# Stores issued alternately by SP and ACT instead of all by SP

## The chip, the core and the metric

The kernel runs on one core of one Trainium2 chip. The metric is the device time of one execution in microseconds (us). A quoted time is the median of a kernel's runs. A quoted ratio is the mean time of one kernel's runs over that of the other's in the same rounds, so it is not quite the ratio of the medians.

The engines are named as the profile names them: PE multiplies, DVE and ACT copy, POOL issues the loads, SP issues stores. Each of these five has its own stream of instructions. Data moves between memory and the core on 16 DMA engines, which all the queues share; they move it in packets, and the trace has one record for each packet. PSUM is the buffer that PE writes its results to.

## The reference

For each of 96 (batch, head) pairs the scores are a product of a 1024x64 and a 64x1024 matrix:

```python
batch, n_heads, seq, head_dim = 8, 12, 1024, 64          # q, k: float32
def reference(q, k):
    return np.einsum('bhid,bhjd->bhij', q, k).astype(np.float32)
```

The inputs are 50 MB in all, the output 403 MB. It is a kernel that mostly writes.

## The kernel before

Heads are handled in batches of four (the first three batches are smaller). POOL loads q and k of a batch and converts them to 16 bits, three batches ahead; PE transposes them into PSUM; DVE copies the transposes out. For each head, 16 matmuls fill eight PSUM tiles, ACT copies five of them and DVE three into one output tile of 4 MB, and one store writes that tile.

```python
in_pool  = ctx.enter_context(tc.tile_pool(name="in_pool", bufs=4))
out_pool = ctx.enter_context(tc.tile_pool(name="out_pool", bufs=4))   # 4 x 4 MB
# ...
        def scores(self, g):
            bh = self.first + g
            # ...
            o_sb = out_pool.tile([P, NT, S], F32, tag="out")
            for t in range(NT):
                # ... two matmuls into ps (L106)
                if t in (1, 4, 6):
                    nc.vector.tensor_copy(out=o_sb[:, t], in_=ps)     # L112
                else:
                    nc.scalar.copy(out=o_sb[:, t], in_=ps)            # L114
            nc.sync.dma_start(                                        # L115
                out=of[bh].rearrange("(p t) j -> p (t j)", p=P),
                in_=o_sb.rearrange("p t j -> p (t j)"),
            )
# ...
        for g in range(b.G):
            b.scores(g)
            if nxt:
                for a in range(g * nxt.G // b.G, (g + 1) * nxt.G // b.G):
                    nxt.transpose(a)        # PE L78, L81, L82; DVE L91, L92
```

Of the kernel before, what the change touches and what calls it, by code (L numbers as in the profile page):

```python
# [1 line left out]

# [5 lines left out]


F16 = mybir.dt.float16  # L10
F32 = mybir.dt.float32
P = 128


@with_exitstack
def kernel(
    ctx: ExitStack,
    tc: tile.TileContext,
    q: bass.AP,
    k: bass.AP,  # L20
    out: bass.AP,
):
    nc = tc.nc

    B, H, S, D = q.shape
    NT = S // P
    BH = B * H
    GMAX = 4
    assert D == 64 and NT == 8 and BH % GMAX == 0





    qf = q.rearrange("b h s d -> (b h s) d")
    kf = k.rearrange("b h s d -> (b h s) d")
    of = out.rearrange("b h i j -> (b h) i j")

    sizes = [1, 1, 2] + [GMAX] * (BH // GMAX - 1)
    assert sum(sizes) == BH  # L40

    consts = ctx.enter_context(tc.tile_pool(name="consts", bufs=1))
    ident = consts.tile([P, P], F16)

    in_pool = ctx.enter_context(tc.tile_pool(name="in_pool", bufs=4))
    tr_pool = ctx.enter_context(tc.tile_pool(name="tr_pool", bufs=2))
    out_pool = ctx.enter_context(tc.tile_pool(name="out_pool", bufs=4))
    pt_pool = ctx.enter_context(
        tc.tile_pool(name="pt_pool", bufs=1, space=bass.MemoryType.PSUM)
    )  # L50
    po_pool = ctx.enter_context(
        tc.tile_pool(name="po_pool", bufs=3, space=bass.MemoryType.PSUM)
    )

    class Batch:
        def __init__(self, first, G):
            self.first, self.G, self.R = first, G, 8 * G

        def load(self):
            rows = slice(self.first * S, (self.first + self.G) * S)  # L60
            self.q_sb = in_pool.tile([P, GMAX * NT, D], F16, tag="q")
            self.k_sb = in_pool.tile([P, GMAX * NT, D], F16, tag="k")
            for src, dst in ((qf, self.q_sb), (kf, self.k_sb)):
                nc.gpsimd.dma_start(  # L64
                    out=dst[:, : self.R],
                    in_=src[rows].rearrange("(p r) d -> p r d", p=P),
                )

        def alloc(self):
            self.qT = tr_pool.tile([P, GMAX * 4 * P], F16, tag="qT")  # L70
            self.kT = tr_pool.tile([P, GMAX * S], F16, tag="kT")

        def transpose(self, a):
            G, pp = self.G, P // self.G
            t_ps = pt_pool.tile([P, 12, P], F16, tag="pt")
            for e in range(4):
                r = a * NT + 2 * e
                nc.tensor.transpose(t_ps[:, e], self.q_sb[:, r : r + 2], ident)  # L78
            for t in range(NT):
                rows = self.k_sb[:, a * NT + t]  # L80
                nc.tensor.transpose(t_ps[0:64, 4 + t], rows, ident)  # L81
                nc.tensor.transpose(t_ps[64:128, 4 + t], rows, ident)  # L82
            qT = self.qT[:, : G * 4 * P].rearrange(
                "c (g e m a) -> c g e m a", g=G, e=4, m=pp
            )
            kT = self.kT[:, : G * S].rearrange(
                "c (g m a t) -> c g m a t", g=G, m=pp, t=NT
            )
            for g in range(G):
                ms = slice(g * pp, (g + 1) * pp)  # L90
                nc.vector.tensor_copy(out=qT[:, g, :, :, a], in_=t_ps[:, 0:4, ms])  # L91
            nc.vector.tensor_copy(  # L92
                out=kT[:, :, :, a],
                in_=t_ps[:, 4:12].rearrange("c t (g m) -> c g m t", g=G),
            )

        def scores(self, g):
            bh = self.first + g
            qT = self.qT.rearrange("c (g e m) -> c g e m", e=4, m=P)
            kT = self.kT.rearrange("c (g j) -> c g j", j=S)  # L100
            o_sb = out_pool.tile([P, NT, S], F32, tag="out")
            for t in range(NT):
                h = (t % 2) * 64
                ps = po_pool.tile([P, S], F32, tag="po")
                for n in range(2):
                    nc.tensor.matmul(  # L106
                        ps[:, n * 512 : (n + 1) * 512],
                        qT[h : h + 64, g, t // 2],
                        kT[h : h + 64, g, n * 512 : (n + 1) * 512],
                    )  # L110
                if t in (1, 4, 6):
                    nc.vector.tensor_copy(out=o_sb[:, t], in_=ps)  # L112
                else:
                    nc.scalar.copy(out=o_sb[:, t], in_=ps)  # L114
            nc.sync.dma_start(  # L115
                out=of[bh].rearrange("(p t) j -> p (t j)", p=P),
                in_=o_sb.rearrange("p t j -> p (t j)"),
            )

    batches, first = [], 0  # L120
    for G in sizes:
        batches.append(Batch(first, G))
        first += G

    AHEAD = 3
    for b in batches[:AHEAD]:
        b.load()
    make_identity(nc, ident)
    batches[0].alloc()
    for a in range(batches[0].G):  # L130
        batches[0].transpose(a)
    for i, b in enumerate(batches):
        if i + AHEAD < len(batches):
            batches[i + AHEAD].load()
        nxt = batches[i + 1] if i + 1 < len(batches) else None
        if nxt:
            nxt.alloc()
# [4 lines that stand above are left out]
                    nxt.transpose(a)  # L142


# [1 line left out]
_INS = ['q', 'k']  # L146
_OUTS = [((8, 12, 1024, 1024), 'float32')]


# [23 lines left out]
```

## Time and profile before

| | before |
|---|---|
| time, median of 4 runs | 1071.33 us (1071.20 to 1072.24) |
| busy share of PE, DVE, ACT | 59%, 53%, 44% |
| DMA queues, share of the 16 engines' span | stores 88.0%, loads 11.9% |

The busy row of the DMA engines in 40 slices, in tenths (9 is 90% or more), and the traffic in each slice:

```profile
DMA  9999999999999999999999999999999999999996
GB/s 213 394 382 386 380 400 414 394 420 396 410 410 384 422 398 410 411 389 419 401 397 424 390 419 401 400 419 389 415 406 399 422 430 430 429 434 432 431 431 292
```

The DMA queues of the same page (packets, MB, share of 16 engines), and the issues by size with the median from issue to landing:

```profile
q1 hardware_dynamic: 13824, 402.66, 88.0%
q0 software_dynamic: 7488, 25.17, 11.9%
...
out_dram<-o_sb SPq DMA_DIRECT2D x96, 4096.0 KB, 36.7
q_sb<-in_q_dram POOLq DMA_DIRECT2D x23, 512.0 KB, 18.1
k_sb<-in_k_dram POOLq DMA_DIRECT2D x23, 512.0 KB, 29.4
```

And the list of waits (total us, times, longest):

```profile
ACT o_sb L114 <- DMA out_dram<-o_sb: 359.1, 87, 7.3
...
DVE o_sb L112 <- DMA out_dram<-o_sb: 213.8, 47, 7.5
ACT o_sb L114 <- PE ps L106: 207.0, 196, 8.9
DVE o_sb L112 <- PE ps L106: 158.8, 165, 2.5
```

Read together: queue q1 (SP's stores) and q0 (POOL's loads) fill the engines' time completely, 88.0% and 11.9%. The engines that compute wait for stores to free one of the four output tiles. A store takes about 10 us of the engines' time, yet 36.7 us from issue to landing, so more than three stores stand in line at any time. Only the last slice is not full. There is no gap that a second queue could fill.

### The profile page before, as it was taken

The numbers are of one execution on the slowest core, as the hardware profiler recorded it, in microseconds if no ns is written. First come the engines' busy times: TensorE is split into PE (matmuls) and PEld (weight loads), VectorE is DVE, ScalarE is ACT, GpSimd is POOL, SyncE is SP. The second block draws the span as 40 slices with busy tenths as digits, with TensorE's granted clock in tenths as the row PEclk, the third lists the DMA queues.
The fourth block names the chain that finished last, engine by engine and source line by source line (L and its number), as shares of the span: only waits on it lengthen the run. The fifth ranks groups of instructions, "written<-read, shape, count | busy, mean of one in ns | idle before, by whom it ended". The sixth has DMA issues, their size and how long they took to land.

```text
span 1069.6 us, 8844 instructions
## 1 busy us (share of the span) xinstructions
PE 627.9 (59%) x3456; PEld 214.0 (20%) x3456; DVE 565.7 (53%) x758; ACT 468.4 (44%) x481; POOL 28.2 (3%) x58
## 2 busy tenths in 40 slices
PE   6786455565654656557465564655656567667530
PEld 2222121121211212212122121221211212212100
DVE  5676445464653646547455464554655646655420
ACT  4454344444533445344443444444444445454530
POOL 3000000000000000000000000000000000000000
PEclk8565555555555555555555555555555555555555
DMA  9999999999999999999999999999999999999996
GB/s 213 394 382 386 380 400 414 394 420 396 410 410 384 422 398 410 411 389 419 401 397 424 390 419 401 400 419 389 415 406 399 422 430 430 429 434 432 431 431 292
DMA packets 21353, 428.39 MB, mean 401 GB/s; under 512 B 2368, under 2 KB 2880, under 8 KB 9024
## 3 DMA queue, kind: packets, MB, share of 16 engines
q1 hardware_dynamic: 13824, 402.66, 88.0%
q0 software_dynamic: 7488, 25.17, 11.9%
q8 instruction: 27, 0.44, 0.1%
q14 instruction: 14, 0.11, 0.0%
HBM read 50.33 MB, written 402.65 MB: 424 GB/s over the span
## 4 chain that ended last, share of the span: by engine, by line
DMA 77%; PE 7%; ACT 7%; DVE 1%; issue 0%; ACTq 0%
DMA out_dram<-o_sb 77%; ACT o_sb L114 7%; PE ps L106 6%; DVE kT L92 0%; DVE qT L91 0%; PE t_ps L81 0%; PE t_ps L78 0%; DVE o_sb L112 0%; PE t_ps L82 0%; ACTq L114 0%
## 5 line engine op out<-in xcount | busy, mean ns | idle before, releaser
L114 ACT COPY o_sb<-ps 128x1024 f32<-128x1024 f32 x480 | 467.1, 1014 | 566.5 <-DMA out_dram<-o_sb 359.1
L106 PE MATMUL ps<-kT,qT 64*128 64x512 f16 x1536 | 480.9, 597 | 270.8 <-ACT o_sb L114 227.2
L112 DVE COPY o_sb<-ps 128x1024 f32<-128x1024 f32 x288 | 351.7, 1223 | 374.0 <-DMA out_dram<-o_sb 213.8
L106 PEld LDWEIGHTS <-qT 64*128 64x128 f16 x1536 | 101.0, 109 | 605.2 <-issue 580.0
L91 DVE COPY qT<-t_ps 128x128 f16<-128x128 f16 (+1 forms) x374 | 121.2, 469 | 95.7 <-PE t_ps L82 95.7
L78 PE MATMUL t_ps<-ident,q_sb 128*128 128x128 f16 x384 | 56.4, 299 | 135.9 <-DVE kT L92 130.2
L92 DVE COPY kT<-t_ps 128x1024 f16<-128x1024 f16 x96 | 118.8, 1237 | 0.0
L81 PE MATMUL t_ps<-ident,k_sb 128*64 128x128 f16 x768 | 102.5, 310 | 0.0
L82 PE MATMUL t_ps<-ident,k_sb 128*64 128x128 f16 x768 | 102.4, 310 | 0.0
L81 PEld LDWEIGHTS <-k_sb 128*64 128x64 f16 x768 | 77.5, 165 | 19.8 <-issue 19.4
L82 PEld LDWEIGHTS <-k_sb 128*64 128x64 f16 x768 | 77.4, 164 | 7.5 <-issue 7.5
L78 PEld LDWEIGHTS <-q_sb 128*128 128x128 f16 x384 | 34.6, 127 | 187.2 <-issue 121.3
L64 POOL DMA_DIRECT2D q_sb<-in_q_dram x26 | 14.0, 537 | 767.5 <-PE t_ps L78 766.8
L64 POOL DMA_DIRECT2D k_sb<-in_k_dram x26 | 13.9, 534 | 13.2 <-PE t_ps L82 13.2
L114 ACT ACT_TABLE_LOAD x1 | 1.3, 1283 | 0.7 <-PEq L157 0.7
masks.py:199 POOL TENSOR_SCALAR_AFFINE_SELECT ident<-ident 128x128 f16<-128x128 f16 x1 | 0.4, 362 | 0.0
masks.py:197 POOL MEMSET ident<- 128x128 f16 x1 | 0.3, 271 | 0.0
L157 POOL MEMSET const-float32-0.0<- 128x1 f32 x1 | 0.1, 98 | 0.2 <-issue 0.2
L157 POOL MEMSET const-bfloat16-1.0<- 128x1 bf16 x1 | 0.1, 101 | 0.0
L157 POOL MEMSET const-uint8-127<- 128x1 uint8 x1 | 0.1, 101 | 0.0
L157 POOL MEMSET const-float32-1.0<- 128x1 f32 x1 | 0.1, 98 | 0.0
## 6 DMA issues: line engine op xcount, KB each, us to landing
out_dram<-o_sb SPq DMA_DIRECT2D x96, 4096.0 KB, 36.7
q_sb<-in_q_dram POOLq DMA_DIRECT2D x23, 512.0 KB, 18.1
k_sb<-in_k_dram POOLq DMA_DIRECT2D x23, 512.0 KB, 29.4
q_sb<-in_q_dram POOLq DMA_DIRECT2D x2, 128.0 KB, 3.5
k_sb<-in_k_dram POOLq DMA_DIRECT2D x2, 128.0 KB, 3.6
q_sb<-in_q_dram POOLq DMA_DIRECT2D x1, 256.0 KB, 6.3
k_sb<-in_k_dram POOLq DMA_DIRECT2D x1, 256.0 KB, 7.0
```

The lines of the kernel that those rows point to most:

```text
L64: nc.gpsimd.dma_start(out=dst[:, : self.R], in_=src[rows].rearrange("(p r) d -> p r d", p=P),)
L78: nc.tensor.transpose(t_ps[:, e], self.q_sb[:, r : r + 2], ident)
L81: nc.tensor.transpose(t_ps[0:64, 4 + t], rows, ident)
L82: nc.tensor.transpose(t_ps[64:128, 4 + t], rows, ident)
L91: nc.vector.tensor_copy(out=qT[:, g, :, :, a], in_=t_ps[:, 0:4, ms])
L92: nc.vector.tensor_copy(out=kT[:, :, :, a], in_=t_ps[:, 4:12].rearrange("c t (g m) -> c g m t", g=G),)
L106: nc.tensor.matmul(ps[:, n * 512 : (n + 1) * 512], qT[h : h + 64, g, t // 2], kT[h : h + 64, g, n * 512 : (n + 1) * 512],)
L112: nc.vector.tensor_copy(out=o_sb[:, t], in_=ps)
L114: nc.scalar.copy(out=o_sb[:, t], in_=ps)
L157: nc = _bacc.Bacc("TRN2", target_bir_lowering=False, num_devices=1)
```

## The change

The intent is to use the queues of two engines for the stores, so that two can be issued and served at once.

```diff
-            nc.sync.dma_start(
+            store = nc.sync if bh % 2 == 0 else nc.scalar
+            store.dma_start(
                 out=of[bh].rearrange("(p t) j -> p (t j)", p=P),
                 in_=o_sb.rearrange("p t j -> p (t j)"),
             )
```

(The copies keep their lines L112 and L114; the store is at L116 after the change.)

## The prediction

> **What bounds the kernel now: the DMA engines.** The row of the page by slices shows DMA at 9 (90% or more) in 39 of 40 slices. In the table by stretches its share is 0.99 to 1.07 from 10 us to 1050 us. The queue view gives stores 88.0% and loads 11.9% of the 16 engines' span: together all of it. The chain that ended last is 77% stores. PE is busy 59%, DVE 53%, ACT 44%; none sets the pace. In the list of waits, ACT waits 359 us and DVE 214 us for a store to free an output buffer. By the packet records, a store costs one engine eight packets of 32 KB at a median of 1.213 us plus a completion write, about 9.72 us. While only stores run (after 840 us) one ends every 9.7 to 9.8 us: no gap is left that a second queue could fill.
>
> **What the change moves.** 48 of the 96 stores of 4 MB go from SP's queue to ACT's; no bytes, packets, copies or matmuls change. SP's waits are 975 us for the DVE copy: it waits for data, not for its own issue cost, so no issue time is saved on the path. The Trainium skill, "DMA: Bandwidth & Descriptors", section "Issuing engines are not separate DMA queues", says that such DMAs "run on the same 16 DMA engines and interleave". This trace, with engines full from one queue, agrees as far as it goes.
>
> **What it adds.** ACT issues 48 stores in program order, each after the DVE copy of t=6. No trace here shows an issue on ACT[...]. A store takes about 11 us with its loads, ACT's copies 5 x 1.01 us of that, so it hides in ACT's wait for buffers.
>
> **The side effect.** Now up to two store queues compete with the load queue. A load pair (q and k, 1 MB) has 16 packets of 0.323 us per engine. Taking turns packet by packet (same page, "Queues, rings and completion order") with one store queue gives 16 x (1.213 + 0.323) = 24.6 us; the trace has 18.1 and 29.4 us to landing, which agrees. With two full store queues it is 16 x (2 x 1.213 + 0.323) = 44 us, about the time of four heads. So loads should land in 40 to 55 us, and the last of them later than 850 us. They are issued over two batches ahead (about 90 to 130 us), so PE should rarely wait; if it does, a store queue empties and the loads get its turn. The sum of work on the engines is unchanged.
>
> Two stores in flight each take twice as long in service but queue half as long; with four buffers the median from issue to landing stays near 36 us.
>
> **Predicted time.** Nearly 0 us of the path goes, nearly 0 is added: 1071 us, 8 in 10 between 1066 and 1077. Chances: faster by over 2%: 0.02; within 2%: 0.94; slower by over 2%: 0.04.
>
> **What would show it.** Right: DMA share still about 1.00 to 1050 us; two hardware queues with about 44% each; 32 KB packets still about 1.21 us; ACT and DVE waits for stores unchanged in sum; load landings longer. The last store's fastest and slowest engines end some 10 us apart before; a much different spread would move the end by a few us.
>
> **What would make it wrong.** Two regions 4 MB apart written at once slow the memory (32 KB packets over 1.25 us); loads starve so far that PE waits and the engines idle; ACT's issue blocks its copies; or a more even spread of the engines at the end saves up to 6 us.

## More of the kernel before

The framework that builds the kernel chooses the order of each engine's instructions itself. The order in the source is only a wish.

## The result, and the profile after

| | before | after |
|---|---|---|
| median, 4 runs each | 1071.33 us | 1075.07 us |
| lowest to highest | 1071.20 to 1072.24 | 1073.43 to 1077.38 |
| ratio, 95% interval | | 1.0035 (1.0015 to 1.0055) |
| profiled execution, span | 1069.6 us | 1071.7 us |

The change costs 0.35%, and the two ranges don't overlap. It is inside the predicted range and inside "within 2%", on its slow side. The profiled execution of the changed kernel was its fastest run, so its profile shows 2.1 us of the 3.7 us.

The same rows, queues and issues of the changed kernel:

```profile
DMA  9999999999999999999999999999999999999998
...
q10 hardware_dynamic: 6912, 201.33, 43.9%
q1 hardware_dynamic: 6912, 201.33, 43.8%
q0 software_dynamic: 7488, 25.17, 12.2%
...
out_dram<-o_sb SPq DMA_DIRECT2D x48, 4096.0 KB, 27.1
out_dram<-o_sb ACTq DMA_DIRECT2D x48, 4096.0 KB, 26.6
q_sb<-in_q_dram POOLq DMA_DIRECT2D x23, 512.0 KB, 25.4
k_sb<-in_k_dram POOLq DMA_DIRECT2D x23, 512.0 KB, 46.2
```

And its waits:

```profile
ACT o_sb L114 <- PE ps L106: 451.8, 258, 11.8
DVE o_sb L112 <- PE ps L106: 226.8, 188, 2.7
...
ACT o_sb L114 <- DMA out_dram<-o_sb: 121.2, 22, 8.2
DVE o_sb L112 <- DMA out_dram<-o_sb: 114.6, 21, 7.9
```

Four things differ. The stores are halved over q1 (SP) and q10 (ACT), as intended. Loads land much later (k in 46.2 us instead of 29.4). The same loads, with the same packets and bytes, take 12.2% of the engines' time instead of 11.9%. And stores land *sooner* after their issue, 27 us instead of 36.7, while ACT waits far less for stores and far more for PE: the line of waiting stores has become shorter.

The last point has a cause that the diff doesn't show. A look at how the compiled streams are ordered (fewer words, no times; x10 means ten of a kind in a row, T one group of transposes copied out) shows two moves in the changed kernel. In ACT's stream, most stores stand behind the *first copy of the next head*; in DVE's stream, three of the four transposes of a batch stand behind a copy of that next head, too:

```
ACT   after:   o_sb x10, store, o_sb x11, store, o_sb x10, store, o_sb x10, store ...
DVE   before:  o_sb x9,  T, T, o_sb x1, qT, o_sb x2, kT, T
DVE   after:   o_sb x10, (T split by one o_sb), o_sb x1, T, T, T       (T = qT copies and one kT copy)
```

A head has five copies on ACT, so from the second store on (after 21 copies, not 20) each store stands one copy late. That copy must wait for a free output tile. The timeline of ACT in the changed kernel (start us, us, what, and in brackets what its idle time waited for) shows a store held for it:

```profile
492.29 1.01 ACT L114 COPY o_sb<-ps 128x1024 f32<-128x1024 f32 x1 [0.93 <-PE ps L106]
497.42 1.01 ACT L114 COPY o_sb<-ps 128x1024 f32<-128x1024 f32 x1 [4.11 <-DMA out_dram<-o_sb]
497.49 0.34 ACTq L116 DMA_DIRECT2D out_dram<-o_sb  x1
```

The last copy of the head ends at 493.30. The store is issued at 497.49, because the next head's first copy stands ahead of it and waits 4.11 us for another store to land. The Trainium skill, "PSUM — Partial Sum Buffer", section "Engine vs sequencer instructions", says that ACT's queue is strictly first in, first out. It says so of the engine's own instructions; in this trace the store, which ACT's sequencer issues, keeps its place as well: it starts 0.07 us after the copy ahead of it has started. Of the 48 stores on ACT, 21 waited over 1 us in this way, 8.28 us at most; all 48 together waited 123 us. The issue itself takes 0.34 us.

DVE's timeline in the changed kernel, just after that, shows the transposes behind the same wait:

```profile
497.46 1.23 DVE L112 COPY o_sb<-ps 128x1024 f32<-128x1024 f32 x1 [3.78 <-DMA out_dram<-o_sb]
...
501.76 1.29 DVE L91 COPY qT<-t_ps 128x128 f16<-128x128 f16 x4 [0.55 <-PE t_ps L82]
502.85 1.25 DVE L92 COPY kT<-t_ps 128x1024 f16<-128x1024 f16 x1
505.80 1.29 DVE L91 COPY qT<-t_ps 128x128 f16<-128x128 f16 x4 [1.71 <-PE t_ps L82]
506.90 1.24 DVE L92 COPY kT<-t_ps 128x1024 f16<-128x1024 f16 x1
509.84 1.29 DVE L91 COPY qT<-t_ps 128x128 f16<-128x128 f16 x4 [1.70 <-PE t_ps L82]
510.94 1.25 DVE L92 COPY kT<-t_ps 128x1024 f16<-128x1024 f16 x1
514.90 1.23 DVE L112 COPY o_sb<-ps 128x1024 f32<-128x1024 f32 x1 [2.72 <-PE ps L106]
```

A head whose tile came free at 497.4 gets its last DVE copy only at 514.9. Counted over 30 to 1030 us, 3.31 stores were outstanding on average before and 2.52 after.

What that does to the DMA engines shows in the table by stretches, first of the changed kernel, then of the kernel before. (The columns after the stretch are busy us of each engine with counts, then the granted clock, the DMA share and GB/s. Loads count there with the 16-bit bytes they write, half of what they read.)

```profile
735.00:740.00 5.00, 4.02 (x16) 1.06 (x13) 2.45 (x2) 3.75 (x4) 0.00 (x0) 0.50 0.99 239
...
860.00:870.00 10.00, 4.99 (x46) 2.77 (x47) 5.57 (x11) 1.11 (x2) 0.00 (x0) 0.50 0.83 356
```

```profile
735.00:740.00 5.00, 3.17 (x10) 0.67 (x10) 1.75 (x2) 2.01 (x3) 0.00 (x0) 0.50 0.98 378
...
860.00:870.00 10.00, 6.53 (x21) 1.40 (x20) 4.41 (x4) 5.65 (x6) 0.00 (x0) 0.50 1.01 436
```

At 735 us the store queues have run almost dry, and most engines work on loads alone: still "busy", at 239 GB/s written instead of 378. At 860 us the last loads are in (861.7 us; 837.5 us before), so nothing fills such a gap any more and the engines idle: a share of 0.83.

The slow load packets of this kernel belong to the same gaps. Of its 3829 load packets that began between 150 and 800 us, 2200 began while fewer than 8 store packets were in flight on the 16 engines (before: 258 of 3807), and those took 339 ns in the mean; the ones that began beside 14 or more took 324 ns.

The packet records of the trace give the sum of it, per engine. Idle in mid-run (16 less the packets in flight, 30 to 1000 us): 2.7 us, before 0. The 4 KB load packets: a mean of 331.8 ns instead of 323.2, which over 368 of them per engine is 3.2 us. The 32 KB store packets: 0.7 us less. The idle at the end: 3.4 us less, because the first and the last engine to finish the last store are 4.4 us apart instead of 10.3. Together +1.8 us, of 2.1 in the spans.

So three suspects were on the table: the stores held in ACT's stream, the order of compute, and the two queues themselves.

### The profile page after: what moved, and what is told of

It reads as the page before. It is cut to its first block, busy times and chain, and to the rows that moved or that the text cites. A ratio compares the mean times of both kernels' runs of the same rounds, so it can differ in the third digit from the quotient of the medians.

```text
span 1071.7 us, 8793 instructions
## 1 busy us (share of the span) xinstructions
PE 662.2 (62%) x3456; PEld 217.8 (20%) x3456; DVE 569.8 (53%) x758; ACT 468.1 (44%) x481; POOL 28.3 (3%) x58
## 3 DMA queue, kind: packets, MB, share of 16 engines
q0 software_dynamic: 7488, 25.17, 12.2%
## 5 line engine op out<-in xcount | busy, mean ns | idle before, releaser
L114 ACT COPY o_sb<-ps 128x1024 f32<-128x1024 f32 x480 | 466.8, 1014 | 573.1 <-PE ps L106 451.8
L106 PE MATMUL ps<-kT,qT 64*128 64x512 f16 x1536 | 513.1, 604 | 218.2 <-ACT o_sb L114 138.2
L112 DVE COPY o_sb<-ps 128x1024 f32<-128x1024 f32 x288 | 350.2, 1222 | 369.2 <-PE ps L106 226.8
L106 PEld LDWEIGHTS <-qT 64*128 64x128 f16 x1536 | 104.3, 111 | 585.9 <-issue 578.6
L91 DVE COPY qT<-t_ps 128x128 f16<-128x128 f16 (+1 forms) x374 | 124.5, 466 | 102.5 <-PE t_ps L82 102.4
## 6 DMA issues: line engine op xcount, KB each, us to landing
q_sb<-in_q_dram POOLq DMA_DIRECT2D x23, 512.0 KB, 25.4
k_sb<-in_k_dram POOLq DMA_DIRECT2D x23, 512.0 KB, 46.2
```

The costliest lines, as they stand in the source:

```text
L91: nc.vector.tensor_copy(out=qT[:, g, :, :, a], in_=t_ps[:, 0:4, ms])
L106: nc.tensor.matmul(ps[:, n * 512 : (n + 1) * 512], qT[h : h + 64, g, t // 2], kT[h : h + 64, g, n * 512 : (n + 1) * 512],)
```

## The experiments

Each pair or group named together ran on one chip, with five rounds. The "32 KB" and "4 KB" columns of the tables are mean durations in ns of the store and the load packets that began between 150 and 800 us, from the packet records of the profiled execution.

### First job: is it the held stores?

E1, label e1_pinned: the changed kernel, with the next head's first ACT copy pinned behind the store.

```diff
-                    nc.scalar.copy(out=o_sb[:, t], in_=ps)
+                    c = nc.scalar.copy(out=o_sb[:, t], in_=ps)
+                    if t == 0:
+                        tc.keep_in_program_order(c)
```

> Stores alternate as in the change, but the next head's first ACT copy is pinned behind the ACT store, so that no finished store waits in ACT's stream for a free buffer (in the change 21 of 48 ACT stores waited over 1 us after their data was ready, 123 us in all; mean stores outstanding 2.5 against 3.3 before). Theory A (held stores let the DMA engines run dry): delay near 0, outstanding back to about 3.3, no idle engines between 800 and 1000 us (2.45 us in the change), and the time 1070 to 1072 us. Theory B (two store queues at once cost the engines something, mainly slower load packets, 3.2 us per engine more than before): the load packets keep a mean near 0.332 us and the time stays at 1074 to 1076 us. Both: about 1073.

E2, label e2_all_act: all stores on ACT, `store = nc.scalar`, held as they are.

> All 96 stores on ACT: one store queue again, but each store still sits behind the next head's first copy in ACT's stream. Theory A: many stores held for several us, outstanding near 2.5 or below, idle DMA engines, 1073 us or more. Theory B: one queue, so load packets back at 0.323 us and 1071 us, holds or not.

E3, label e3_all_act_pinned: E2 with the pin of E1.

> All 96 stores on ACT, each ahead of the next head's first copy: one queue and no hold. Both theories: as before, 1071 us within 1 us. A third theory, that ACT's issue of about 0.34 us itself costs time: above 1072.5 us, as there are twice as many of them as in the change.

E4, label e4_swapped: the changed kernel with `store = nc.scalar if bh % 2 == 0 else nc.sync`.

> As the change with the queues swapped: even heads on ACT, odd heads on SP. In the change the held stores were those of every fourth head (the last of a batch of four, an odd one); that one is now on SP. Theory A: few holds (under 30 us in all), outstanding over 2.8, time at most 1073 us. Theory B: 1074 to 1076 us as in the change, load packets near 0.332 us.

| | store queues | held in ACT, us in all | median us | ratio to before (95%) | 32 KB on SP, ACT | 4 KB |
|---|---|---|---|---|---|---|
| before | 1 | 0 | 1070.89 | | 1225, - | 322 |
| E1 pinned | 2 | 0 | 1076.48 | 1.0056 (1.0043 to 1.0068) | 1219, 1229 | 337 |
| E2 all ACT | 1 | 65 | 1070.13 | 0.9991 (0.9978 to 1.0005) | -, 1224 | 322 |
| E3 all ACT, pinned | 1 | 0 | 1071.77 | 1.0002 (0.9989 to 1.0014) | -, 1224 | 322 |
| E4 swapped | 2 | 181 | 1081.61 | 1.0093 (1.0080 to 1.0106) | 1230, 1246 | 323 |

("Held" leaves out the ordinary 0.03 us from data ready to issue.) Theory A, the held stores, falls. Without any hold E1 is as slow as the change or slower, and with holds but one queue E2 is as fast as before. The short line of stores is not the cause either: E2 and E3 have 2.42 and 2.44 stores outstanding, as few as E1 with 2.44. Nor is it ACT's issue: E3 has twice as many and costs nothing that can be measured. What E1 and E4 share, and E2 and E3 lack, is two store queues.

E1 and E3 are nearly a clean pair for an order about as late as the changed kernel's. Neither holds a store, their DVE streams agree in 747 of 758 places, and PE's differ by a few matmuls within each batch. E1, with two queues, takes 1076.18 to 1078.43 us; E3, with one, 1069.72 to 1072.63. Of E1's load packets between 150 and 800 us 2001 of 3834 began beside fewer than 8 store packets, of E3's 147 of 3840.

E4 was a surprise in size, +0.93%, and in its holds (under 30 us were expected). Its load packets were not slow, against what theory B said; its store packets were. Its loads landed in 91.1 (q) and 112.6 us (k). So two queues cost in two forms: slow load packets and gaps in the change and E1, slow store packets in E4.

### Second job: queues against order of compute

The order of PE's and DVE's instructions had changed in each of these kernels, since the framework reorders them whenever a store moves. So the next four kernels pin every matmul, transpose and DVE copy to the order of the source, and the compiled streams of PE and DVE are then the same in both kernels of a pair. In the "late" pair all four transposes of the next batch stand behind the copies t=0 and t=1 of the batch's first head, like in the changed kernel but more so; in the "even" pair one stands after each head, as the source has it.

```diff
+    K = tc.keep_in_program_order
-                nc.tensor.transpose(t_ps[:, e], self.q_sb[:, r : r + 2], ident)
+                K(nc.tensor.transpose(t_ps[:, e], self.q_sb[:, r : r + 2], ident))
     ... (the same around every matmul, transpose and DVE copy; ACT's t=0 copy as in E1)
# late pair only:
+                if t == 1 and nxt:            # in scores(), for the batch's first head
+                    for a in range(nxt.G):
+                        nxt.transpose(a)
# E5, E7:
-            store = nc.sync if bh % 2 == 0 else nc.scalar
+            store = nc.sync
```

> The order of PE's and DVE's instructions is pinned, the same in this kernel and the next: all four transposes of the next batch stand behind the copies t=0 and t=1 of a batch's first head, so they wait for an output buffer. All stores on SP. Theory C (two store queues served in turns land their stores in close pairs, so buffers come back late; this costs time only where the compute of the next head is also late, since then the engines run out of stores): one queue hides the late order, 1070 to 1072 us, outstanding stores near 2.4. Theory D (two store queues and the load queue in turns cost engine time whatever the compute order): also 1070 to 1072 us. A theory O, that the order of compute which the change brought along is the cause and the queues are not: 1074 us or more.

> As the kernel before it in this job, with stores alternating between SP and ACT; nothing else differs. Theories C and D: 1074 to 1079 us, engines idle or running on loads alone at each fourth head. Theory O: as the one-queue kernel of the same order, within 1 us.

> The order is pinned as the program is written: one transpose group after each head, so all heads take about the same time. All stores on SP. All theories: 1070 to 1072 us.

> The same even order, stores alternating. Theory C: heads come evenly, the store queues do not run dry, at most 1.5 us over the one-queue kernel of the same order. Theory D: 3 to 6 us over it, as with the late order. Theory O: the same as it.

| | order | store queues | median us (lowest to highest) | ratio to before (95%) | 32 KB on SP, ACT | 4 KB |
|---|---|---|---|---|---|---|
| E5 | late | 1 | 1070.98 (1068.34 to 1074.69) | 1.0004 (0.9988 to 1.0021) | 1226, - | 323 |
| E6 | late | 2 | 1073.02 (1072.19 to 1074.40) | 1.0019 (1.0007 to 1.0031) | 1220, 1229 | 334 |
| E7 | even | 1 | 1069.99 (1067.73 to 1072.72) | 0.9991 (0.9977 to 1.0005) | 1221, - | 323 |
| E8 | even | 2 | 1080.70 (1077.82 to 1083.89) | 1.0089 (1.0073 to 1.0105) | 1228, 1247 | 322 |

Theory O (order of compute alone) falls: with one queue the late and the even order both run as before. Theory C (paired landings need a late head to do harm) can't be the whole cause: the even order, where heads come regularly and 3.3 stores are outstanding on average, suffers most. For the late orders it is not excluded: there the engines do run short of stores (idle in mid-run 2.7 us in the change, 6.2 us in E1, 3.6 us in E6, against 1.0 us in E5). Theory D (the queues cost time whatever the order) fits best. E7 and E8 differ in nothing but the queue of every second store, and differ by 10.8 us (the means of their runs, 1069.93 and 1080.71). The late pair differs by 1.5 us in the mean, less than E5's own spread, so there the effect is not told from noise. E5's two longest runs, 1074.69 (the profiled one) and 1074.35 us, are also the two whose granted TensorE clock was high, 0.90 and 0.86 against 0.51 to 0.58; the other four average 1070.2 us. Whether the clock made them longer was not tested.

The DMA queues of E7:

```profile
q1 hardware_dynamic: 13824, 402.66, 88.0%
q0 software_dynamic: 7488, 25.17, 11.9%
...
q_sb<-in_q_dram POOLq DMA_DIRECT2D x23, 512.0 KB, 17.4
k_sb<-in_k_dram POOLq DMA_DIRECT2D x23, 512.0 KB, 28.5
```

and of E8:

```profile
q10 hardware_dynamic: 6912, 201.33, 44.3%
q1 hardware_dynamic: 6912, 201.33, 43.8%
q0 software_dynamic: 7488, 25.17, 11.8%
...
q_sb<-in_q_dram POOLq DMA_DIRECT2D x23, 512.0 KB, 75.0
k_sb<-in_k_dram POOLq DMA_DIRECT2D x23, 512.0 KB, 96.1
```

The engines are full in both, and none idles in mid-run. By the packet records the store queues take 938.7 us of each engine's time in E7 (88.0% of its span of 1066.8 us) and 948.4 us in E8 (88.1% of 1076.0 us). The same packets and bytes cost each engine 9.7 us more, and the span is 9.2 us longer. Most of the loss sits on ACT's queue: 476.6 us, where half of E7's stores take 469.4.

The packet records say which packets those are. In E8 between 150 and 800 us, 1113 of ACT's 3742 store packets took over 1233 ns, against 89 of SP's 3743, and 159 of 7588 in E7. Of the slow ones on ACT's queue, 99% ended within 12 ns of the start of a load packet; of ACT's ordinary ones 86% did so too. Of SP's ordinary packets, 89% ended where a packet of ACT's queue started. (A moment picked at random lies that close to such a start in some 13% of cases.) So the engines go round: SP's store packet, ACT's, a load packet, SP's again. The Trainium skill, "DMA: Bandwidth & Descriptors", section "Queues, rings and completion order", says that each engine takes its queues in turn, packet by packet, and the traces agree: k, issued 1 us after q, has 8 packets of its own on each engine, and it lands 12.2 us after q in E7, where 8 x (1.221 + 0.322) is 12.3 us, and 22.1 us after q in E8, where 8 x (1.228 + 1.247 + 0.322) is 22.4. Sixteen such rounds, 44.8 us for a load pair, are about the time of four heads (a pair lands every 44.7 us in E8, and every 44.1 us in E7 too). Loads in E8 get no more than their turn and it is just what they need, so about two pairs are in line and k lands in 96.1 us.

### Third job: take the loads away

If two streams of stores, 4 MB apart, simply disturbed each other in memory, they would do so without loads. These four kernels give wrong results: from the seventh batch on they use the inputs of the fourth to sixth again, so that most of the run has stores alone. (Twenty of the 26 pairs of loads are gone; the expectation says 18, which was a slip.)

```diff
         def load(self):
             rows = slice(self.first * S, (self.first + self.G) * S)
+            if self.first >= 16:
+                old = batches[3 + (self.first // 4 - 4) % 3]
+                self.q_sb, self.k_sb = old.q_sb, old.k_sb
+                return
```

(The input pool has six buffers instead of four, so that these inputs stay.)

> Wrong result on purpose: from the seventh batch on the inputs of the fourth to sixth are used again, so all loads end early (18 of 26 load pairs are gone) and the rest of the run has stores alone. Even order of compute, one store queue on SP. All theories: the stores' own time, 96 x 9.72 us plus start, early loads and end, about 975 us; 32 KB packets at 1.213 us.

> As the kernel before it, stores alternating (with loads this change of queue cost 9 us of span: 32 KB packets on ACT's queue took 1.239 us in the mean, nearly all slow ones just ahead of a load packet). Theory E (two store queues cost where they share the engines with loads): within 1.5 us of the one-queue kernel, packets at 1.213 us on both queues. Rival F (two store streams 4 MB apart slow each other at the memory, loads or not): 5 us or more slower.

> Without the later loads, late order of compute, one store queue. Stores alone have no loads to fill gaps: where a head comes late and fewer than two stores are left, engines idle. One queue: 975 to 985 us.

> As the kernel before it, stores alternating. Theory E alone: as the one-queue kernel within 1.5 us. If two stores served in turns also run dry together (landing in pairs, so that a buffer comes back later): 3 to 10 us slower, all of it as idle engines and none as slower packets.

| | order | store queues | median us (lowest to highest) | 32 KB on SP, ACT |
|---|---|---|---|---|
| E9 | even | 1 | 979.11 (978.98 to 979.35) | 1220, - |
| E10 | even | 2 | 979.33 (978.60 to 979.56) | 1220, 1220 |
| E11 | late | 1 | 991.11 (989.80 to 991.12) | 1221, - |
| E12 | late | 2 | 989.36 (989.19 to 989.78) | 1235, 1219 |

The DMA queues of E9:

```profile
q1 hardware_dynamic: 13824, 402.66, 96.0%
q0 software_dynamic: 1728, 4.20, 2.4%
```

and of E10:

```profile
q1 hardware_dynamic: 6912, 201.33, 48.1%
q10 hardware_dynamic: 6912, 201.33, 47.9%
q0 software_dynamic: 1728, 4.20, 2.4%
```

Without loads, the 10.8 us between E7 and E8 shrink to 0.2 us between E9 and E10, and the packets are as fast on two queues as on one. Rival F falls: in the even order the cost needs two store queues *and* the loads. Whether it is the loads' turns on the engines or their reads of memory beside two regions of writes isn't told apart, since E9 and E10 lack both. In the late pair, too, two queues are not slower without loads, but 1.8 us faster. It says one thing more. With one queue, the late order costs 12 us without loads (979.11 to 991.11) and nothing with them (1069.99 and 1070.98). The loads fill the gaps that a late head leaves, and so hide them.

Several expectations missed in size. E6 came out below its 1074 to 1079 us; E8 lost 10.8 us instead of 3 to 6; E9 took 4 us more than its 975 us, and E11 6 us more than the upper end of its range; E12 was faster than E11 by more than the 1.5 us allowed, and no theory said so.

## Why the prediction was right, and where it wasn't

- **Right: the bound, and no gain to be had.** The engines were full from one queue, and the page of the changed kernel shows them as full from two. The range and the class held. That the time fell into the range owes something to luck: with the same stores alternating, E4 (queues swapped) took 1081.61 us and E8 (even order) 1080.70 us, both outside 1066 to 1077, and the prediction did not know which order of compute the framework would choose.
- **Right: the queues' shares of about 44%, the median store packet at 1.213 us, ACT's issue hidden** (0.34 us each), **loads landing later, and the last of them after 850 us** (861.7 us). Of the loads only k lies in the named 40 to 55 us (46.2); q lands in 25.4, since by the prediction's own turns its 8 packets need half of the 44 us. The check of these turns in the prediction, 24.6 us against landings of 18.1 and 29.4, fits loosely; the step from q's landing to k's fits closely: 12.2 us before and 21.9 after, where 8 turns are 12.3 and 22.0.
- **Off: "nearly 0 is added".** The step that failed is "The sum of work on the engines is unchanged". The bytes and packets are unchanged, their time is not. In the changed kernel 4 KB load packets took 3.2 us more per engine; in E8, where both store queues are always filled, store packets took 9.8 us more. The experiments show that in the even order two store queues and loads together are needed for this (E7 with E8, E9 with E10); that two store queues cost time in a late order, too, E1 and E3 show nearly as cleanly. The added time was put at nearly 0 and measured 3.7 us, idle time included, and 10.8 us in the even order.
- **Off: the median from issue to landing "stays near 36 us", and "ACT and DVE waits for stores unchanged in sum".** They were 27 us, and 236 us (121.2 and 114.6) instead of 573. The step that failed is that nothing but the queue would move. The framework put ACT's stores behind a copy that waits, and moved DVE's transposes behind another; E2, E3 and E5 show that neither costs time while one queue serves the stores. Where the order was held the same, the landing did stay: 38.0 us in E7, 37.0 and 37.8 us in E8.
- **Half right: "if it does, a store queue empties and the loads get its turn".** They do, at 735 us, but at 239 GB/s written, and after the last load the gap is idle time.
- **The hoped-for gain at the end came and was eaten.** The engines' ends drew together, from 10.3 to 4.4 us, which is worth 3.4 us at the end by the idle count. The span grew all the same.

What stays open: why three in ten store packets on ACT's queue are slow in E8, when only 2% are in E7, where 45% end at the start of a load packet as well; whether it is ACT's queue or its place in the round, just before the loads; and why the SP queue of E12 has slow packets (1235 ns) and no loss of time. In the changed kernel itself, the division into slow loads and idle time is read from one trace and was not tested apart; E8 loses its time in another form, so it does not prove how the changed kernel loses its own. No version beat the kernel before: E2 and E7 are at 0.9991 of it, and both intervals include 1.

## What to carry to other kernels

When the DMA engines are full from one queue, a second issuing engine for the same transfers has nothing to win, and beside the stream of loads it cost 0.2% to 0.9% here; the queue table can show this as a larger share of time for the same packets and bytes. A DMA put in a computing engine's stream can move other instructions and get held behind one that waits, so compare the compiled order before you blame the hardware, and pin the order when you test one thing. A transfer that fills gaps hides them: judge an order of compute also by what it costs without its filler.

## What the Trainium skill lacked or had wrong

- "DMA: Bandwidth & Descriptors", section "Issuing engines are not separate DMA queues": it says that issuing from several engines only saves the sequencer's issue time. That it can also cost time is missing: 1069.99 to 1080.70 us (E7, E8) with the same order of compute, packets and bytes, and 979.11 to 979.33 us (E9, E10) when most loads are gone.
- The same page, section "Queues, rings and completion order": taking turns is confirmed (k lands 22.1 us after q in E8, worked out as 22.4), but what the turns do to the time until a transfer lands isn't said: the median landing of the k loads went from 28.5 to 96.1 us.
- The same page gives no sign that the same packet takes longer on one queue than on another: 1113 of 3742 store packets on ACT's queue were over 1233 ns in E8, 89 of 3743 on SP's, and 159 of 7588 in E7.
- No page that was read warns that a DMA in a computing engine's stream can be held behind a waiting instruction. "PSUM — Partial Sum Buffer" states strict order for ACT's queue, but not that a DMA issue keeps its place in it: 21 of 48 stores were held over 1 us, 8.28 us at most.
